# A two-layer encoder on one core: matmuls in runs by width, toeplitz biases in the grid biases' buffers, last halves by token half

## The chip, the core and the metric

The kernel runs on one core of a Trainium2 chip. The metric is the device time of one execution in microseconds (us), lower is better. Before the change it is 2096.45 us, the median of three runs (2096.22 to 2096.68).

## What is computed

The input is 256 tokens of 2048 float32 features. Each of two layers normalises, projects, attends, projects back with a residual, normalises again and applies a squared-ReLU MLP (2048 to 8192 to 2048) with a residual. A final normalisation ends it. Layer 0 has 16 heads of 128: eight with a neighbourhood on a 64-wide grid and a learned bias, eight with a mix of dilated bands. Layer 1 has 16 query heads on four key and value heads, a band of 128 tokens to each side and a sink in each head's softmax. Cut to what matters:

```python
for i in range(DEPTH):                      # 2
    h = rms_norm(x, attn_norm[i])
    if i % 2 == 0:
        x = x + even_mixer(h, even_w_in, even_rpb, even_w_out)   # grid heads | dilated heads
    else:
        x = x + odd_mixer(h, odd_w_qkv, odd_sink, odd_w_out)     # banded, with sink
    h = rms_norm(x, mlp_norm[i])
    a = relu(h @ w_mlp_in[i])
    x = x + (a * a) @ w_mlp_out[i]
return rms_norm(x, final_norm)
```

## The kernel before

**Two parts for each number.** Each float32 operand of a large product is split into a high part in a matmul format of TensorE (ScalarE, L90) and the rest, the low part (VectorE, L91). A product is high x high + high x low + low x high. The code calls the parts of a weight h and l; u holds both parts of the normalised input (feature-major: 16 k-tiles of 128 features, high then low, 256 tokens each), hid those of the MLP's hidden layer, o those of the attention's output.

**Units.** A unit makes 128 output features of a projection by features. For each of the 16 k-tiles there is a pair: h as the stationary operand against 512 columns, u high and low side by side (L143), and l against the 256 columns of u high (L141). Both accumulate in one PSUM tile, acc, of which there are three. `products` issues one pair and `k_range` loops over k; the order in the pair turns round on every odd k, so the widths go 512, 256, 256, 512, 512, 256, 256 and so on. A `tick` comes after every fourth pair. `two_units` holds back the last four k-tiles of two units until waiting work is done.

**Chunks.** A chunk makes 512 output columns of a product by tokens (the values, the output projections, the second MLP matrix). Here the weights are the moving operand, 512 wide, and the stationary operand is one of the two token halves of 128: for each k, and for each token half, three 512-wide matmuls (L185). Even chunks accumulate in acc, odd ones in s_ps. A chunk of the MLP has 32 k-tiles, two to a weight load.

**Weights.** `take_half` (L103 to L111) keeps loads of 512 KB ("halves") flowing: SP issues the load into raw (six buffers), ScalarE makes h and VectorE l (five buffers each).

**Order.** The program is written as one stream; small steps of the attention are put in by `later(steps, fn)`, due after so many ticks: scores (L296), then the softmax, transposes of the weights (L321), then the values (L340). LAGS_0, LAGS_1 and LAGS_END hold the steps between these. When the program is built, instructions are put on each engine's queue when their data and buffers are expected to be free; each engine then runs its queue strictly in order. So a step with few inputs can stand in a queue well ahead of its place in the code.

**Biases of layer 0.** The grid heads (0 to 7) get their bias from a table that GpSimd loads (rev, L533) and expands (rel, L538, four buffers). The other eight get a toeplitz bias, one VectorE operation on a constant table tabs (L374, tile toep, two buffers of 128x384). tabs is loaded by GpSimd behind the bias of head 4 (L543), and so are the rows of x for the residual (L547). Layer 1 uses the same function on another part of the table.

**Start.** TensorE is warmed by ten small products of ones (L467). Then gx (gains and x by features) and the first weights (`first`, four units' worth) come in alternating loads on SP, two k-tiles at a time (L482, L484), with k = 0 and k = 1 apart. Four units are computed side by side in four PSUM tiles, k outermost (L501 to L504). Each k-tile of u is made from gx by L200 (high) and L201 (low).

**End.** In the last chunk of layer 1's MLP all matmuls of both token halves finish together. Then `added` adds both halves (L397), squares follow on ScalarE (L206), `finish_norm` makes the scale of each token (L225 to L232), `scaled` applies it in eight pieces on ScalarE and VectorE (L426, L428, L430), and SP stores four column chunks of 512 KB, both token halves in each (L437).

Of the kernel before, what the change touches and what calls it, by code (L numbers as in the profile page):

```python
# [43 lines left out]
def encoder(ctx: ExitStack, tc: tile.TileContext, a: dict, out: bass.AP):  # L44
# [34 lines left out]

    nc.vector.memset(ones, 1.0)  # L80
# [56 lines left out]
    def products(ps, h, l, k, flip):  # L137

        for low in (flip, not flip):
            if low:  # L140
                nc.tensor.matmul(ps[:, :T], l, u[:, k, 0, :], start=False, stop=k == KT - 1 and not flip)  # L141
            else:
                nc.tensor.matmul(ps, h, u[:, k].rearrange("p a t -> p (a t)"), start=k == 0,  # L143
                                 stop=k == KT - 1 and flip)
# [25 lines left out]
    def chunk(act, nk, c, done, before=None):  # L170

        if c % 2 == 0:
            ps = [acc_ps.tile([P, NC], F32, name="acc") for _ in range(2)]
        else:
            ps = [aux_ps.tile([P, NC], F32, name="s_ps", bufs=2) for _ in range(2)]
        for k in range(nk):
            if k % 2 == 0:
                parts = [w.rearrange("p k c -> p (k c)") for w in take_half()]
            if before and k == nk - 2:
                before()  # L180
            h, l = (w[:, (k % 2) * NC:(k % 2 + 1) * NC] for w in parts)
            for j in range(2):
                js = slice(j * P, (j + 1) * P)
                for n, (x, y) in enumerate(((0, h), (0, l), (1, h))):
                    nc.tensor.matmul(ps[j], act[:, k, x, js], y, start=k == 0 and n == 0,  # L185
                                     stop=k == nk - 1 and n == 2)
            tick()
        done(c, ps)
# [35 lines left out]
    def finish_norm():  # L224
        nc.vector.tensor_reduce(ms, ssq, axis=AX.X, op=ALU.add)  # L225
        r0, v, e = (work.tile([P, 2], F32, name=n, bufs=1) for n in ("r0", "v", "e"))
        nc.scalar.activation(r0, ms, AF.Sqrt, bias=eps, scale=1.0 / D)
        nc.vector.tensor_scalar(v, ms, 1.0 / D, EPS, op0=ALU.mult, op1=ALU.add)
# [3 lines left out]
        nc.vector.scalar_tensor_tensor(rcol, e, 1.5, r0, op0=ALU.add, op1=ALU.mult)  # L232
# [40 lines left out]
    def value_quad(pool, keep):  # L273

        def done(_, ps):
            assert norm["ready"]
            w = pool.tile([P, 2, 2, NC], F32R, name="v", bufs=1)
            for j in range(2):
                nc.scalar.activation(w[:, 0, j, :], ps[j], AF.Copy, scale=rcol[:, j:j + 1])
                nc.vector.scalar_tensor_tensor(w[:, 1, j, :], ps[j], rcol[:, j:j + 1],  # L280
                                               w[:, 0, j, :].bitcast(F32), op0=ALU.mult, op1=ALU.subtract)
            keep.append(w)
        chunk(u, KT, 0, done)
# [67 lines left out]
    def project_out(o, which):  # L351
        def done(c, ps):
# [12 lines left out]
        for c in range(CHUNKS):  # L365
            chunk(o, KT, c, done, before if c == 0 else None)
            if c == 2:
                warm(AF.Sqrt, ssq[:, 0, 0:1])
        heads_done.clear()

    def toeplitz(pool, slope, which):
        def fn():
            t = pool.tile([P, TW], F32, name="toep", bufs=2)
            nc.vector.scalar_tensor_tensor(t, tabs[:, 0, :], -slope, tabs[:, which, :],  # L374
                                           op0=ALU.mult, op1=ALU.add)
            return [t[:, P - P * i:P - P * i + T] for i in range(2)]
        return fn

    def mlp(layer, which_next):
        with tc.tile_pool(name=f"mlp{layer}", bufs=1) as pool:  # L380
# [3 lines left out]
            for b in range(2):  # L384
# [9 lines left out]
                def added(c, ps):  # L394
                    cs = slice(c * NC, (c + 1) * NC)
                    for j in range(2):
                        nc.vector.scalar_tensor_tensor(xs[:, j, cs], ps[j], rsq[:, j:j + 1], xs[:, j, cs],  # L397
                                                       op0=ALU.mult, op1=ALU.add)
                    if b == 1 and which_next < 4:
                        to_features(c, which_next)  # L400
                    for j in range(2):
                        if b == 1:
                            squares(c, j)
                    if b == 1 and which_next == 4 and c < CHUNKS - 1:
                        nc.vector.tensor_mul(xs[:, :, cs], xs[:, :, cs],
                                             last_gain[:, None, cs].to_broadcast([P, 2, NC]))

# [12 lines left out]
    def last_norm(last_gain):  # L420
        finish_norm()

        def scaled(c, j, engine):
            y, r = xs[:, j, c * NC:(c + 1) * NC], rcol[:, j:j + 1]
            if c == CHUNKS - 1:
                nc.vector.scalar_tensor_tensor(y, y, r, last_gain[:, c * NC:], op0=ALU.mult, op1=ALU.mult)  # L426
            elif engine is nc.scalar:
                nc.scalar.activation(y, y, AF.Copy, scale=r)  # L428
            else:
                nc.vector.tensor_scalar(y, y, r, None, op0=ALU.mult)  # L430

        for c, engines in ((0, (nc.scalar, nc.scalar)), (3, (nc.vector, nc.vector)),
                           (1, (nc.vector, nc.scalar)), (2, (nc.vector, nc.vector))):
            cs = slice(c * NC, (c + 1) * NC)
            for j in range(2):
                scaled(c, j, engines[j])
            nc.sync.dma_start(out[:, :, cs], xs[:, :, cs])  # L437
# [28 lines left out]
    for _ in range(10):  # L466
# [5 lines left out]
    rs = []  # L472
# [4 lines left out]
    for k0 in range(0, KT, 2):  # L477
        r = raw.tile([P, 2, 4, P], F32, name="r")
        for k1 in ((k0 + 1, k0 + 2) if k0 == 0 else (k0 + 2,)):
# [4 lines left out]
            nc.sync.dma_start(r[:, ks.start - k0:ks.stop - k0], a["first"][:, ks])  # L484
# [3 lines left out]
        rs.append(r)  # L488
# [4 lines left out]
    nc.gpsimd.tensor_scalar(sink_neg, sink, -1.0, None, op0=ALU.mult)  # L493
    for k0 in range(0, KT, 2):
# [174 lines left out]
```

## Time and profile before

| | before |
|---|---|
| median of three runs | 2096.45 us |
| profiled execution, its own time | 2096.66 us |
| its span, first to last instruction | 2094.8 us |
| TensorE busy | 2066.0 us (99%) |
| VectorE, ScalarE, GpSimd busy | 1261.1, 1016.0, 23.4 us |
| TensorE's mean granted clock over the span | 0.995 |
| 512-wide matmuls of units, L143, outside the start | 2864 |
| their 256-wide partners, L141 | 2864 |
| 512-wide matmuls of the MLP's chunks, L185 on hid | 3072 |
| HBM read and written | 386.46 and 2.10 MB |

In the profile PE is TensorE's matmul and PEld its weight load, DVE is VectorE, ACT ScalarE, POOL GpSimd and SP the engine that issues most loads. Times are in us from the start of the span, unless marked ns. A timeline row has the start, the length, the engine, the line, the operation, the tile written and those read, the shape, and how many were merged (x2); in square brackets stands the engine's idle time just before and who ended it. A row of the waits has who waited, for whom, the total, the number of times and the longest. A row of the stretches has the stretch, its length, the busy time and count of engines, TensorE's granted clock (1.00 is full), the share of the DMA engines and the GB/s. The length of a matmul in the rows is from its start to the end of its results, longer than the distance to the next start; the spacing is read from the starts.

### The profile page before, as it was taken

The numbers are of one execution on the slowest core, as the hardware profiler recorded it, in microseconds if no ns is written. First come the engines' busy times: TensorE is split into PE (matmuls) and PEld (weight loads), VectorE is DVE, ScalarE is ACT, GpSimd is POOL, SyncE is SP. The second block draws the span as 40 slices with busy tenths as digits, with TensorE's granted clock in tenths as the row PEclk, the third lists the DMA queues.
The fourth block names the chain that finished last, engine by engine and source line by source line (L and its number), as shares of the span: only waits on it lengthen the run. The fifth ranks groups of instructions, "written<-read, shape, count | busy, mean of one in ns | idle before, by whom it ended". The sixth has DMA issues, their size and how long they took to land.

```text
span 2094.8 us, 27875 instructions
## 1 busy us (share of the span) xinstructions
PE 2066.0 (99%) x10712; PEld 1759.4 (84%) x10712; DVE 1261.1 (60%) x1777; ACT 1016.0 (48%) x1453; POOL 23.4 (1%) x42
## 2 busy tenths in 40 slices
PE   9799999999999999999999999999999999999997
PEld 7688888888888888888888888888888888888886
DVE  7567765566654456665545887566664446665453
ACT  7455555554543344554444655554543334544442
POOL 2200000000000000000000000000000000000000
PEclk9999999999999999999999999999999999999999
DMA  9655555555566655555555544565566665556662
GB/s 321 192 166 168 176 175 172 182 189 190 191 192 191 192 192 190 191 189 193 185 190 188 163 151 146 186 201 191 189 190 194 191 194 188 190 191 192 191 193 98
DMA packets 107812, 390.38 MB, mean 186 GB/s; under 512 B 12144, under 2 KB 12416, under 8 KB 107040
## 3 DMA queue, kind: packets, MB, share of 16 engines
q1 hardware_dynamic: 106496, 383.87, 57.4%
q0 software_dynamic: 1184, 4.74, 0.7%
q8 instruction: 84, 1.38, 0.3%
q14 instruction: 48, 0.39, 0.1%
HBM read 386.46 MB, written 2.10 MB: 185 GB/s over the span
## 4 chain that ended last, share of the span: by engine, by line
PE 97%; DMA 1%; POOL 0%; DVE 0%; ACT 0%; issue 0%; SPq 0%; DVEq 0%; POOLq 0%
PE acc L143 32%; PE acc L185 25%; PE s_ps L185 21%; PE acc L141 16%; PE m_ps L340 1%; PE s_ps L296 1%; DMA rev<-in_rpb 1%; PE p_ps L321 1%; PE m_ps L214 1%; POOL rel L538 0%; DMA r<-in_first 0%; DMA tabs<-in_tabs 0%; PE s_ps L143 0%; POOL rev L533 0%; DVE l L91 0%
## 5 line engine op out<-in xcount | busy, mean ns | idle before, releaser
L91 DVE TENSOR_TENSOR l<-r,h 128x1024 fp32r<-128x1024 f32 (+1 forms) x721 | 882.9, 1225 | 615.4 <-ACT h L90 602.9
L90 ACT ACTIVATE h<-r 128x1024 fp32r<-128x1024 f32 (+1 forms) x721 | 761.9, 1057 | 689.5 <-PE acc L185 274.5
L143 PE MATMUL acc<-u,h 128*128 128x512 f32 x2864 | 915.4, 396 | 1.3 <-ACT h L90 1.3
L141 PEld LDWEIGHTS acc<-u,l 128*128 128x128 f32 x2864 | 538.1, 188 | 125.0 <-DVE l L91 1.2
L141 PE MATMUL acc<-u,l 128*128 128x256 f32 x2864 | 566.4, 278 | 0.5 <-DVE l L91 0.5
L143 PEld LDWEIGHTS acc<-u,h 128*128 128x128 f32 x2864 | 442.8, 189 | 2.1 <-ACT h L90 1.6
L185 PE MATMUL s_ps<-h,hid 128*128 128x512 f32 x1024 | 318.3, 390 | 0.0
L185 PE MATMUL acc<-h,hid 128*128 128x512 f32 x1024 | 317.5, 389 | 0.0
L185 PEld LDWEIGHTS acc<-h,hid 128*128 128x128 f32 x1024 | 192.2, 188 | 39.9
L185 PEld LDWEIGHTS s_ps<-h,hid 128*128 128x128 f32 x1024 | 192.2, 188 | 39.8
L192 ACT ACTIVATE t<-acc 128x256 f32<-128x256 f32 x179 | 68.9, 385 | 292.6 <-PE acc L143 291.6
L185 PE MATMUL s_ps<-l,hid 128*128 128x512 f32 x512 | 199.2, 389 | 0.0
L185 PE MATMUL acc<-l,hid 128*128 128x512 f32 x512 | 199.2, 389 | 0.0
L194 DVE TENSOR_TENSOR z<-acc,t 128x256 f32<-128x256 f32 x179 | 75.9, 425 | 146.7 <-ACT t L192 146.3
L185 PEld LDWEIGHTS s_ps<-l,hid 128*128 128x128 f32 x512 | 96.1, 188 | 19.7
L185 PEld LDWEIGHTS acc<-l,hid 128*128 128x128 f32 x512 | 96.1, 188 | 19.7
L185 PE MATMUL acc<-h,u 128*128 128x512 f32 x320 | 102.9, 394 | 0.7 <-ACT h L90 0.7
L185 PE MATMUL acc<-h,o 128*128 128x512 f32 x256 | 82.9, 394 | 0.0
L185 PE MATMUL s_ps<-h,o 128*128 128x512 f32 x256 | 82.7, 395 | 0.0
L185 PEld LDWEIGHTS acc<-h,u 128*128 128x128 f32 x320 | 59.8, 188 | 13.0 <-ACT h L90 1.0
L185 PE MATMUL acc<-l,u 128*128 128x512 f32 x160 | 62.6, 391 | 0.5 <-DVE l L91 0.5
L390 DVE SCALAR_TENSOR_TENSOR z<-z 128x256 f32<-128x256 f32 x128 | 54.4, 425 | 4.3
(100 smaller groups left out, 1027.6 us busy)
## 6 DMA issues: line engine op xcount, KB each, us to landing
r<-in_w_mlp_in SPq DMA_DIRECT2D x256, 512.0 KB, 4.1
r<-in_w_mlp_out SPq DMA_DIRECT2D x256, 512.0 KB, 3.7
r<-in_even_w_in SPq DMA_DIRECT2D x56, 512.0 KB, 3.8
r<-in_odd_w_qkv SPq DMA_DIRECT2D x40, 512.0 KB, 3.8
r<-in_even_w_v SPq DMA_DIRECT2D x32, 512.0 KB, 3.7
r<-in_even_w_out SPq DMA_DIRECT2D x32, 512.0 KB, 3.6
r<-in_odd_w_out SPq DMA_DIRECT2D x32, 512.0 KB, 3.6
r<-in_odd_w_v SPq DMA_DIRECT2D x8, 512.0 KB, 3.6
```

What stands on the lines that cost most here:

```text
L90: nc.scalar.activation(hi, src, AF.Copy)
L91: nc.vector.tensor_sub(lo, src, hi.bitcast(F32))
L141: nc.tensor.matmul(ps[:, :T], l, u[:, k, 0, :], start=False, stop=k == KT - 1 and not flip)
L143: nc.tensor.matmul(ps, h, u[:, k].rearrange("p a t -> p (a t)"), start=k == 0, stop=k == KT - 1 and flip)
L185: nc.tensor.matmul(ps[j], act[:, k, x, js], y, start=k == 0 and n == 0, stop=k == nk - 1 and n == 2)
L192: nc.scalar.activation(t, ps[:, T:], AF.Copy)
L194: nc.vector.tensor_add(z, ps[:, :T], t)
L214: nc.tensor.transpose(ps[:, k, j * P:(j + 1) * P], xs[:, j, (k0 + k) * P:(k0 + k + 1) * P], ident)
L296: nc.tensor.matmul(s_ps[:, i, :], qh[:, x, qs], kh[:, y, :], start=n == 0, stop=n == 2)
L321: nc.tensor.transpose(p_ps[:, j, i * P:(i + 1) * P], s[:, i, j * P:(j + 1) * P], ident)
L340: nc.tensor.matmul(o_ps[:, :T], vv[:, x, j, side * P:(side + 1) * P], pt[:, y, j, :], start=n == 0, stop=n == 5)
L390: nc.vector.scalar_tensor_tensor(z, z, 0.0, z, op0=ALU.max, op1=ALU.mult)
```

## The change

Four things are done.

1. `products` takes a list of pairs and issues all matmuls of one width, then all of the other, with a tick behind each. `k_range` gives it eight k-tiles at a time: the first eight high (512 wide) first, the second eight low (256 wide) first. So a unit is 8 high, 16 low, 8 high. At the start one call covers two k-tiles of the four units, high first for k = 0 and 1, low first for k = 2 and 3, and so on in turn.
2. Toeplitz biases of layer 0 take a buffer of the name rel, with four buffers, in the place of toep. Layer 1 keeps toep.
3. In the last chunk of the program, the last four halves (eight k-tiles) are taken all four, and their products made for the first token half, which is then finished (added, squared, normalised, stored), and then for the second. `finish_norm` works on one token half's column. The output of each token half leaves in two stores: the upper 1024 columns by SP, the lower ones by ScalarE's queue. The columns 0 to 1023 are scaled by ScalarE, the others by VectorE.
4. The very first weight load is issued by ScalarE's queue, as its first instruction. Eight products of ones are made in the place of ten.

```diff
+    r = raw.tile([P, 2, 4, P], F32, name="r")
+    nc.scalar.dma_start(r[:, 0:1], a["first"][:, 0:1])
+    rs = [r]
     nc.vector.memset(ones, 1.0)
...
-    def products(ps, h, l, k, flip):
-
-        for low in (flip, not flip):
-            if low:
-                nc.tensor.matmul(ps[:, :T], l, u[:, k, 0, :], start=False, stop=k == KT - 1 and not flip)
-            else:
-                nc.tensor.matmul(ps, h, u[:, k].rearrange("p a t -> p (a t)"), start=k == 0,
-                                 stop=k == KT - 1 and flip)
+    def products(banks, tiles, k, low_first, last):
+
+        for low in (low_first, not low_first):
+            for n, (ps, (h, l)) in enumerate(zip(banks, tiles)):
+                stop = last and low != low_first and (k[n] == KT - 1)
+                if low:
+                    nc.tensor.matmul(ps[:, :T], l, u[:, k[n], 0, :], start=False, stop=stop)
+                else:
+                    nc.tensor.matmul(ps, h, u[:, k[n]].rearrange("p a t -> p (a t)"), start=k[n] == 0, stop=stop)
+            tick()
 
     def k_range(ps, parts, ks):
-        for k in ks:
-            h, l = parts[k]
-            products(ps, h, l, k, k % 2 == 1)
-            if k % 4 == 3:
-                tick()
+        for k0 in range(ks.start, ks.stop, HALF):
+            k = range(k0, min(k0 + HALF, ks.stop))
+            products([ps] * len(k), [parts[i] for i in k], k, k0 >= HALF, True)
...
-    def chunk(act, nk, c, done, before=None):
+    def chunk(act, nk, c, done, before=None, apart=0):
...
-        for k in range(nk):
+        for k in range(nk - 2 * apart):
...
+        if apart:
+            kept = [take_half() for _ in range(apart)]
             for j in range(2):
-                js = slice(j * P, (j + 1) * P)
-                for n, (x, y) in enumerate(((0, h), (0, l), (1, h))):
-                    nc.tensor.matmul(ps[j], act[:, k, x, js], y, start=k == 0 and n == 0,
-                                     stop=k == nk - 1 and n == 2)
-            tick()
-        done(c, ps)
+                for k in range(nk - 2 * apart, nk):
+                    some(kept[(k - nk) // 2], k, (j,))
+                done(c, ps, (j,))
+        else:
+            done(c, ps, range(2))
...
     def toeplitz(pool, slope, which):
         def fn():
-            t = pool.tile([P, TW], F32, name="toep", bufs=2)
+
+            if which == 1:
+                t = pool.tile([P, 6, GRID], F32, name="rel", bufs=4).rearrange("p j c -> p (j c)")
+            else:
+                t = pool.tile([P, TW], F32, name="toep", bufs=2)
...
-                    chunk(hid, 2 * KT, c, added)
-            if which_next == 4:
-                last_norm(last_gain)
+                    chunk(hid, 2 * KT, c, added, apart=4 if which_next == 4 and b == 1 and c == CHUNKS - 1 else 0)
+
+    def last_norm(j, last_gain):
+
+        finish_norm(slice(j, j + 1))
+        r = rcol[:, j:j + 1]
+        for c in range(CHUNKS):
+            y = xs[:, j, c * NC:(c + 1) * NC]
             if c == CHUNKS - 1:
                 nc.vector.scalar_tensor_tensor(y, y, r, last_gain[:, c * NC:], op0=ALU.mult, op1=ALU.mult)
+            elif c == CHUNKS - 2:
+                nc.vector.tensor_scalar(y, y, r, None, op0=ALU.mult)
+            else:
                 nc.scalar.activation(y, y, AF.Copy, scale=r)
+        nc.sync.dma_start(out[:, j, D // 2:], xs[:, j, D // 2:])
+        nc.scalar.dma_start(out[:, j, :D // 2], xs[:, j, :D // 2])
...
-    for _ in range(10):
+    for _ in range(8):
         nc.tensor.matmul(wps[:, :P], ones, ones, start=True, stop=True)
...
+            if k1 > 1:
+                nc.sync.dma_start(r[:, ks.start - k0:ks.stop - k0], a["first"][:, ks])
...
-        for k in range(k0, k0 + 2):
-            for i in range(4):
-                products(sps[i], h[:, k - k0, i, :], l[:, k - k0, i, :], k, k > 0 and i % 2 == 1)
+        which = [(k, i) for k in range(2) for i in range(4)]
+        products([sps[i] for _, i in which], [(h[:, k, i, :], l[:, k, i, :]) for k, i in which],
+                 [k0 + k for k, _ in which], k0 % 4 == 2, True)
```

More of the change, by code (lines that the diff above doesn't have):

```diff
@@ L222, in encoder, with finish_norm @@
     norm = {"ready": False, "waiting": []}
[L224 to L228, printed above, removed]
+    def finish_norm(js=slice(0, 2)):
+        r0, v, e = (work.tile([P, 2], F32, name=n, bufs=1)[:, js] for n in ("r0", "v", "e"))
+        m, r = ms[:, js], rcol[:, js]
+        nc.vector.tensor_reduce(m, ssq[:, js], axis=AX.X, op=ALU.add)
+        nc.scalar.activation(r0, m, AF.Sqrt, bias=eps, scale=1.0 / D)
+        nc.vector.tensor_scalar(v, m, 1.0 / D, EPS, op0=ALU.mult, op1=ALU.add)
         nc.vector.reciprocal(r0, r0)
@@ L273, in value_quad, with done @@
     def value_quad(pool, keep):
-        def done(_, ps):
+        def done(_, ps, js):
             assert norm["ready"]
@@ L351, in project_out, with done @@
     def project_out(o, which):
-        def done(c, ps):
+        def done(c, ps, js):
             cs = slice(c * NC, (c + 1) * NC)
@@ L392, in hidden, with added @@
                     return fn
-                def added(c, ps):
+                def added(c, ps, js):
                     cs = slice(c * NC, (c + 1) * NC)
-                    for j in range(2):
+                    for j in js:
                         nc.vector.scalar_tensor_tensor(xs[:, j, cs], ps[j], rsq[:, j:j + 1], xs[:, j, cs],
                                                        op0=ALU.mult, op1=ALU.add)
-                    if b == 1 and which_next < 4:
+                    if b == 0:
+                        return
+                    if which_next < 4:
                         to_features(c, which_next)
[L401 to L404, printed above, removed]
+                    for j in js:
+                        squares(c, j)
+                    if which_next == 4 and c < CHUNKS - 1:
                         nc.vector.tensor_mul(xs[:, :, cs], xs[:, :, cs],
                                              last_gain[:, None, cs].to_broadcast([P, 2, NC]))
+                    elif which_next == 4:
+                        last_norm(js[0], last_gain)
                 for j in range(0, 2 * KT, 2):
@@ L493, in encoder @@
     nc.gpsimd.tensor_scalar(sink_neg, sink, -1.0, None, op0=ALU.mult)
+    assert not tasks
     for k0 in range(0, KT, 2):
```

34 lines of the change are left out of this document (14 added, 20 removed).

## The prediction

> **What bounds the kernel now.** I read the page first. Its first lines and the chain by engine:
>
> ```profile
> span 2094.8 us, 27875 instructions
> PE 2066.0 (99%) x10712; PEld 1759.4 (84%) x10712; DVE 1261.1 (60%) x1777; ACT 1016.0 (48%) x1453; POOL 23.4 (1%) x42
> PE 97%; DMA 1%; POOL 0%; DVE 0%; ACT 0%; issue 0%; SPq 0%; DVEq 0%; POOLq 0%
> ```
>
> TensorE carries 97% of the chain, so only three things can move the time: the spacing of its matmuls, the places where it stands still, and what is left when it has ended. For the spacing I read the chain in order of time (start, length, what) and one group of the page:
>
> ```profile
> 146.73 1.43 PE m_ps L340 x12
> 721.24 43.52 PE s_ps L185 x192
> 943.10 43.52 PE acc L185 x192
> ```
>
> ```profile
> L141 PEld LDWEIGHTS acc<-u,l 128*128 128x128 f32 x2864 | 538.1, 188 | 125.0 <-DVE l L91 1.2
> ```
>
> In a chunk all matmuls are 512 wide: 43.52/192 = 0.2267 us each. Twelve 256-wide ones in a row take 1.43/12 = 0.119. Between the chunks (721.24 + 43.52 = 764.76, and 943.10) lie the 32 units of the second half of layer 0's MLP: 178.34/32 = 5.573 us for one unit's 16 pairs of 512 (h) and 256 (l). At the uniform prices it would be 16 x 0.2267 + 16 x 0.119 = 5.531. So the present order, with eight changes to 256 and back per unit, costs 0.042 us a unit. The group, the weight loads of the 256-wide matmuls, gives the number of pairs outside the start: 2864, or 179 units.
>
> For the stillstands I read the waits, which hold one large one for TensorE, and around it the timelines of the engines concerned:
>
> ```profile
> PE m_ps L340 <- DVE v L280: 11.0, 1, 11.0
> DVE toep L374 <- DMA tabs<-in_tabs: 12.0, 1, 12.0
> ```
>
> ```profile
> 59.72 0.40 PE L340 MATMUL m_ps<-pt,v 128*128 128x256 f32 x2
> 71.16 2.52 PE L340 MATMUL m_ps<-pt,v 128*128 128x256 f32 x10 [11.04 <-DVE v L280]
> ```
>
> ```profile
> 55.07 0.61 DVE L314 TENSOR_SCALAR s<-s,rd 128x256 f32<-128x256 f32 x2
> 67.68 0.56 DVE L374 SCALAR_TENSOR_TENSOR toep<-tabs 128x384 f32<-128x384 f32 x1 [12.01 <-DMA tabs<-in_tabs]
> 68.15 1.22 DVE L91 TENSOR_TENSOR l<-r,h 128x1024 fp32r<-128x1024 f32 x1
> 69.29 0.69 DVE L91 TENSOR_TENSOR pt<-p_ps,pt 128x512 fp32r<-128x512 f32 x1
> ...
> 70.35 1.41 DVE L280 SCALAR_TENSOR_TENSOR v<-acc,rcol,v 128x512 fp32r<-128x512 f32 x2
> ```
>
> VectorE's queue is in order, and a toeplitz bias of head 8, used much later, stands in it at 55.7 us, waiting for the table, whose load was issued only then:
>
> ```profile
> 63.15 0.57 POOL L543 DMA_DIRECT2D tabs<-in_tabs  x1
> ```
>
> Behind it stand an l split, a pt and the value split v, for which TensorE waits. The stretches of TensorE (busy, count, granted clock) show a second price:
>
> ```profile
> 59.90:64.30 4.40, 0.22 (x2) 1.00 0.06 11
> 64.30:71.10 6.80, 0.00 (x0) 0.50 0.99 368
> 71.10:74.60 3.50, 3.44 (x14) 0.50 0.76 261
> ```
>
> After 4.4 idle us the clock was at half, and stayed so through 3.44 us of matmuls.
>
> **The change part by part.** *Toeplitz in the grid buffers.* What put L374 so early? A free buffer: the trace shows a later one directly behind the last read that frees its buffer.
>
> ```profile
> 118.78 0.09 DVE L301 DVE_READ_ACCUMULATOR2_ANT st<- 128x1 f32 x1
> ...
> 192.80 0.08 DVE L301 DVE_READ_ACCUMULATOR2_ANT st<- 128x1 f32 x1
> 192.92 0.56 DVE L374 SCALAR_TENSOR_TENSOR toep<-tabs 128x384 f32<-128x384 f32 x1
> ```
>
> Now it has to have one of the four grid buffers, and heads 4 to 7, ahead of it in the code, claim them first; head 8 gets the buffer of head 4, which is read to 118.8 (the first row), 50 us behind the landing of the table. The 59.96 to 71.16 hole, 11.2 us, goes, and half of 3.44 us at half clock, less what the partial start hid: 1.6. What is late next? ScalarE's half of v:
>
> ```profile
> 57.84 1.38 ACT L279 ACTIVATE v<-acc,rcol 128x512 fp32r<-128x512 f32 x2 [0.56 <-PE acc L185]
> ```
>
> The first v tile is there at about 58.55; VectorE, free from 55.7, has had 2.9 us by then for the l split and the pt (1.22 + 0.69), and has the low half of the first v at 59.3 and of the second at 60.0 (1.41 for both). TensorE wants the first at 59.96 and the second at 60.3. I take the whole 12.8; between the ends 11.2 (clock price not returned) and 12.8.
>
> *Runs by width.* A unit becomes 8 h, 16 l, 8 h, so 16 of each width in a row across units, with one change and back instead of eight. What does one cost when the runs are long? The nearest place is a block of six 256s between 512s:
>
> ```profile
> 128.99 0.88 PE L296 MATMUL s_ps<-k,q 128*128 128x256 f32 x6
> 129.70 0.39 PE L185 MATMUL acc<-h,u 128*128 128x512 f32 x1
> ...
> 130.86 0.62 PE L185 MATMUL acc<-h,u 128*128 128x512 f32 x2
> ```
>
> Five 512s start from 129.70 to before 130.86: 1.16 us, against 5 x 0.2267 = 1.133: the first ones behind a narrow run are slower by 0.027 together. So one change and back costs 0.03 here and 0.042/8 = 0.005 in the present mixture. A unit becomes 5.531 + 0.005 to 0.03 = 5.536 to 5.561, and 179 units save 6.6 to 2.1 us. The inserted block is nearer to a long run than the mixture: 2.5 us. Were 256s a little dearer in long runs (0.120), it would be none.
>
> The Trainium skill (TensorE: Matmul & The Clock Gate, Back-to-back issue gap) gives an isolated gap of N/2.4 + 2.5 ns whatever stands beside the matmul. By it the order is worth nothing, and the sum below is 2.5 us smaller; this trace has 227 ns where it gives 216.
>
> Ticks stay four to a unit but fall behind 8 h (1.81 us) or 8 l (0.95), not every 1.39; each lag of the attention shifts by at most 0.45 us. I put no cost, 0 to 2 us for the range. The insertions of six now fall between runs of the two widths.
>
> *Start.* TensorE waits here for the second weights (rows in time; the first is the load that changes queue):
>
> ```profile
> 1.18 0.42 SPq L484 DMA_DIRECT2D r<-in_first  x1
> 9.25 1.06 ACT L90 ACTIVATE h<-r 128x1024 fp32r<-128x1024 f32 x1 [0.33 <-DMA r<-in_first]
> 10.34 1.23 DVE L91 TENSOR_TENSOR l<-r,h 128x1024 fp32r<-128x1024 f32 x1 [0.90 <-ACT h L90]
> 10.36 0.73 PE L143 MATMUL acc<-u,h 128*128 128x512 f32 x2 [1.30 <-ACT h L90]
> 11.62 0.50 PE L141 MATMUL acc<-u,l 128*128 128x256 f32 x2 [0.53 <-DVE l L91]
> ```
>
> With k = 2, 3 low first, TensorE starts at the end of L91 (11.6), not of L90: one idle stretch of 2.5 us instead of 1.30 + 0.53. Against that SP issues one load less, so this chain moves up by about 0.4; ScalarE, which now issues that load ahead of its table load, has nothing to do before 3 us. The eight warm-ups instead of ten end earlier, and the wait covers it. Net zero, from -0.8 to +1.
>
> *End.* Rows of the last chain:
>
> ```profile
> 2081.26 1.43 DVE L397 SCALAR_TENSOR_TENSOR gx<-s_ps,rsq,gx 128x512 f32<-128x512 f32 x2 [10.60 <-PE s_ps L185]
> 2082.80 0.63 ACT L206 ACTIVATE sq<-gx 128x512 f32<-128x512 f32 x1
> 2084.67 0.16 DVE L232 SCALAR_TENSOR_TENSOR rcol<-e,r 128x2 f32<-128x2 f32 x1
> 2084.87 1.95 ACT L428 ACTIVATE gx<-gx,rcol 128x512 f32<-128x512 f32 x3 [0.82 <-DVE rcol L232]
> 2084.87 1.42 DVE L426 SCALAR_TENSOR_TENSOR gx<-gx,rcol,last_gain 128x512 f32<-128x512 f32 x2
> 2086.28 3.53 SPq L437 DMA_DIRECT2D out<-gx  x4
> ```
>
> and stretches of the stores (length, clock, DMA share, GB/s):
>
> ```profile
> 2088.30:2089.40 1.10, 0.50 1.02 382
> 2093.50:2094.80 1.30, 0.50 0.00 0
> ```
>
> The second L397 starts with the end of the matmuls (2081.9), and the steps to rcol stay as long for one column. Then 2 MB leave at 382 GB/s, 1.38 us per 512 KB. The first half's chain takes the same 4.4 us (2081.9 to 2086.28), but starts 24 x 0.2267 = 5.4 us before the end of the matmuls; its two stores, issued 1 us before that end, are gone before the second half's are issued 4.4 us behind it. So two stores remain of four: 2 x 1.38 = 2.8 us less, and VectorE's two scalings, one of them the shorter kind without the gain, release the first issue up to 0.2 earlier. Two queues share the one path: no more. 3.0, from 2.6 to 3.3. ScalarE issues its first store between its scalings and the second squares, 1 us before they are due; nobody waits. The four kept halves fit the five buffers; their splits are long done (VectorE idle 10.60 above).
>
> Sum: 12.8 + 2.5 + 0 + 3.0 = 18.3. The profiled execution took 2096.66 us (span 2094.8 and 1.9 around it), the median 2096.45: 2078.4 and 2078.2.
>
> **The rivals.** (1) *Order is free*, as by the rule above: 2078.2 + 2.5 = 2080.7. For it: 256s that grow to 0.120. (2) *The toeplitz still gets in early*, into a free grid buffer ahead of head 5's bias: two of four are free at 55 us, since only heads 0 and 1 have been read. Against: the code claims head 5's first. The 12.8 stay: 2091.0. (3) *The 512s do not settle*: the five above average 0.232; if all do, a unit is 5.531 + 16 x 0.0053 = 5.616, 0.043 over now, 7.7 us: 2078.2 + 2.5 + 7.7 = 2088.4. Against: the chunk rows settle. (4) *The start's idle stretch halves the clock*. 4.4 us did, 1.3 did not; 2.1 to 2.5 lies between. The low clock lasted 10.3 us (64.3 to 74.6); half of that is 5.1: 2083.3. The Trainium skill (same page, The HAM clock gate) asks for a whole idle window of 3.4 us; the trace agrees so far. (5) *Slower: weight loads bound the runs of l*. A load is recorded at 0.188 us (the group above), longer than the 0.119 of the matmul that must cover it. Twelve in a row ran well; if from the thirteenth on each takes 0.188, a unit pays 4 x 0.069 = 0.276, 49 us in all: 2080.7 + 49 = 2130. It decides from 15.8/179 = 0.088 us a unit, two such matmuls.
>
> **How the numbers follow.** Forecast 65%, (1) 14%, (2) 9%, (3) 5%, (4) 5%, (5) 2%. The forecast's own ends are 2078.2 - 4.1 (runs at 6.6) - 0.8 - 0.3 = 2073, and 2078.2 + 2.5 + 1 + 2 + 0.4 = 2084. Range 2072 to 2086: it takes in (1) and (4), and leaves out (2), (3), (5), 16%, and some tail. 0.2% is 4.2 us, about what a measurement of this kernel can tell from no change. Faster by that: all but (5) and the poor ends of (2) and (3): 0.93; within it 0.05; slower 0.02.
>
> **What would show it.** No wait of VectorE on the table, L374 first behind 100 us, TensorE without a hole at 60 to 71 us and the clock at full from 7 us to the end; a second-half MLP of 177.2 to 178.0 us between the chunks instead of 178.34; one hole near 9 to 11.6 us, no longer than 2.6; from the last matmul to the end of the span 10 us instead of 12.9. The prediction is wrong if a hole above 1 us stands at the first values, if the stretch of units is longer than now, or if the stores still queue behind one another for more than two transfers.

## The result, and the profile after

Four runs of the changed kernel took 2079.56 us in the median (2079.34 to 2082.51), beside 2096.56 (2096.22 to 2099.78) for the kernel before. The ratio is 0.9919, with a 95% interval of 0.9902 to 0.9936: 17.0 us less, where the forecast was 18.3. The profiled execution took 2079.34 us with a span of 2077.2, that is 2.1 us around the span where the kernel before had 1.9.

The first lines of the page of after and its chain by engine:

```profile
span 2077.2 us, 27861 instructions
PE 2063.3 (99%) x10708; PEld 1767.9 (85%) x10708; DVE 1257.6 (61%) x1782; ACT 1014.3 (49%) x1455; POOL 27.8 (1%) x42
PE 99%; DMA 0%; ACT 0%; DVE 0%; SPq 0%; issue 0%
```

TensorE now carries 99% of the chain instead of 97%. Its busy time fell by only 2.7 us: most of the gain is time in which it stood still.

Where the time went can be read by following one and the same matmul through both traces, since the products outside the start and the last halves stand in nearly the same order. The table gives the starts, in us:

| matmul | before | after | gained so far |
|---|---|---|---|
| first product of the start | 5.33 | 5.17 | 0.16 |
| first matmul of the first value chunk | 31.68 | 30.88 | 0.80 |
| first unit behind that chunk | 58.33 | 58.36 | -0.03 |
| first matmul of the next value chunk | 121.68 | 108.89 | 12.79 |
| last matmul of all | 2081.52 | 2067.58 | 13.94 |
| end of the span | 2094.84 | 2077.19 | 17.65 |

**The hole.** The timelines of VectorE and of TensorE in after, around the first values, and one row of the stretches (length, busy time and count of TensorE, clock, DMA share, GB/s):

```profile
57.64 0.68 DVE L94 TENSOR_TENSOR pt<-p_ps,pt 128x512 fp32r<-128x512 f32 x1
58.59 1.44 DVE L296 SCALAR_TENSOR_TENSOR v<-acc,rcol,v 128x512 fp32r<-128x512 f32 x2 [0.28 <-ACT v L295]
```

```profile
58.36 1.99 PE L148 MATMUL acc<-u,h 128*128 128x512 f32 x8
60.19 1.60 PE L356 MATMUL m_ps<-pt,v 128*128 128x256 f32 x12
61.63 2.08 PE L146 MATMUL acc<-u,l 128*128 128x256 f32 x16
```

```profile
59.70:71.20 11.50, 11.50 (x73) 1.00 0.69 213
```

VectorE reaches the value split at 58.59, with 0.28 us of waiting for ScalarE, where it did so at 70.35 before. The products of the weights with the values, now L356, run from 60.19 without a gap. The toeplitz biases, now L394, come much later. The row has the shortest, median and longest duration in ns and the first and last start in us:

```profile
L394 DVE SCALAR_TENSOR_TENSOR rel<-tabs x8: 535/558/560, 106.3 to 241.1; 128x384 f32<-128x384 f32 x8
```

**Runs by width.** The chain of after, in order of time, around the second half of layer 0's MLP:

```profile
708.13 43.52 PE s_ps L186 x192
755.38 3.65 PE acc L148 x16
760.94 3.65 PE acc L148 x16
766.51 3.65 PE acc L148 x16
...
929.78 43.52 PE acc L186 x192
```

Sixteen 512s in a row take 3.65 us, and a unit 760.94 - 755.38 = 5.56. By the starts of the matmuls the 32 units take 178.13 us, where they took 178.34.

**The clock at the start.** Stretches of after, cut where its granted clock can change:

```profile
8.85:12.26 3.41, 2.16 (x13) 1.00 1.04 407
29.33:32.74 3.41, 1.87 (x8) 1.00 0.74 289
32.74:36.15 3.41, 3.41 (x10) 0.50 0.79 250
36.15:39.57 3.42, 3.42 (x16) 1.00 0.73 215
```

The clock was at half from 32.74 to 36.15 us, which is new in this place. What leads to it are two waits at the beginning of the first value chunk:

```profile
30.88 0.73 PE L186 MATMUL acc<-h,u 128*128 128x512 f32 x2 [1.01 <-ACT h L93]
32.13 0.50 PE L186 MATMUL acc<-l,u 128*128 128x512 f32 x1 [0.53 <-DVE l L94]
```

**The end.** Rows of the timeline of after:

```profile
2068.00 0.75 DVE L417 SCALAR_TENSOR_TENSOR gx<-s_ps,rsq,gx 128x512 f32<-128x512 f32 x1 [1.45 <-PE s_ps L186]
2070.64 0.16 DVE L248 SCALAR_TENSOR_TENSOR rcol<-e,r 128x1 f32<-128x1 f32 x1
2070.84 1.33 ACT L452 ACTIVATE gx<-gx,rcol 128x512 f32<-128x512 f32 x2 [0.81 <-DVE rcol L248]
2071.24 0.74 DVE L448 SCALAR_TENSOR_TENSOR gx<-gx,rcol,last_gain 128x512 f32<-128x512 f32 x1
2072.21 0.34 ACTq L454 DMA_DIRECT2D out<-gx  x1
```

and the groups of the stores, first of before (duration of the issue in ns, first and last start), then of after:

```profile
L437 SPq DMA_DIRECT2D out<-gx x4: 602/724/1218, 2086.3 to 2088.6; - x4
DMA to landing us min/median/max: 3.2/4.2/5.0
```

```profile
L453 SPq DMA_DIRECT2D out<-gx x2: 343/344/344, 2066.6 to 2072.0; - x2
L454 ACTq DMA_DIRECT2D out<-gx x2: 338/342/347, 2066.8 to 2072.2; - x2
DMA to landing us min/median/max: 2.6/3.2/3.7
```

The last matmul ends at 2067.97, and the span 9.23 us later, where it was 12.93.

### The profile page after: what moved, and what is told of

The parts are those of the page before. It is cut to its first block, busy times and chain, and to the rows that moved or that the text cites. A ratio compares the mean times of both kernels' runs of the same rounds, so it can differ in the third digit from the quotient of the medians.

```text
span 2077.2 us, 27861 instructions
## 1 busy us (share of the span) xinstructions
PE 2063.3 (99%) x10708; PEld 1767.9 (85%) x10708; DVE 1257.6 (61%) x1782; ACT 1014.3 (49%) x1455; POOL 27.8 (1%) x42
## 3 DMA queue, kind: packets, MB, share of 16 engines
q8 instruction: 84, 1.38, 0.3%
## 4 chain that ended last, share of the span: by engine, by line
PE 99%; DMA 0%; ACT 0%; DVE 0%; SPq 0%; issue 0%
PE acc L148 31%; PE acc L186 26%; PE s_ps L186 21%; PE acc L146 16%; PE s_ps L312 1%; PE m_ps L356 1%; PE p_ps L337 1%; PE m_ps L229 1%; DMA r<-in_first 0%; PE s_ps L148 0%; DVE l L94 0%; ACT h L93 0%; PE s_ps L146 0%; ACT gx L452 0%; SPq L500 0%; PE m_ps L259 0%
## 5 line engine op out<-in xcount | busy, mean ns | idle before, releaser
L148 PE MATMUL acc<-u,h 128*128 128x512 f32 x2864 | 694.2, 391 | 0.3 <-DVE u L216 0.3
L148 PEld LDWEIGHTS acc<-u,h 128*128 128x128 f32 x2864 | 524.1, 188 | 100.4 <-ACT h L93 0.6
L146 PEld LDWEIGHTS acc<-u,l 128*128 128x128 f32 x2864 | 366.9, 191 | 14.0 <-DVE l L94 1.9
L146 PE MATMUL acc<-u,l 128*128 128x256 f32 x2864 | 377.0, 283 | 1.7 <-DVE l L94 1.7
```

Of the source, the lines that this page charges most:

```text
L146: nc.tensor.matmul(ps[:, :T], l, u[:, k[n], 0, :], start=False, stop=stop)
L148: nc.tensor.matmul(ps, h, u[:, k[n]].rearrange("p a t -> p (a t)"), start=k[n] == 0, stop=stop)
```

## The experiments

The theory: the hole was one blocked queue and goes whole; the order of the widths is worth what each change from one width to the other costs, which the runs can measure; the end is one path of bytes; and the start moves by a clock that falls after a thin stretch. The rivals: the hole's gain is partly due to something else; the order is free; the end is set by a price per store; the start's loss comes from the new order of products in it. Beside the times, each kernel's trace is compared matmul by matmul with that of before, since one execution's start differs from the next by more than a microsecond.

**The toeplitz buffers alone**, in the kernel before:

```diff
-            t = pool.tile([P, TW], F32, name="toep", bufs=2)
+            if which == 1:
+                t = pool.tile([P, 6, GRID], F32, name="rel", bufs=4).rearrange("p j c -> p (j c)")
+            else:
+                t = pool.tile([P, TW], F32, name="toep", bufs=2)
```

> The kernel before with one edit alone: layer 0's toeplitz biases take a buffer of the name rel. My theory: the whole hole of TensorE at 60 to 71 us came from the bias standing early in VectorE's queue, so it goes with this edit alone, and the half-clock stretch behind it: 2096.6 - 12.8 = 2083.8 us, no wait of VectorE on the table, and the next stages unmoved. Rival: a part of the 12.8 us in the changed kernel came from the new tick places or from the start (other edits); then a hole or a wait above 0.5 us stays near 60 us here, and the time is above 2084.5.

Measured: 2084.30 us (2083.18 to 2085.35), beside 2097.80 for the kernel before; ratio 0.9936 (0.9920 to 0.9953), 13.5 us. In the trace the step across the hole is 12.84 us; from there on no stage differs by more than 0.03. So edit 2 alone gives the 12.8, and the hole's price is independent of the other edits. One thing was not foreseen: the first value chunk began 1.60 us later than before, although the start of this kernel is the old one. Its stretches:

```profile
8.16:11.57 3.41, 1.70 (x8) 1.00 1.01 378
11.57:14.99 3.42, 3.21 (x11) 0.50 1.04 414
32.05:35.47 3.42, 2.17 (x10) 1.00 0.34 123
```

Here the clock fell at the first wait of the start, with code that kept it at full in the trace of before, and stayed at full behind the second (the third row). The fall is thus no property of the new order.

**The change with the old order of the widths**, in the units and at the start:

```diff
...
     def k_range(ps, parts, ks):
...
+        for k in ks:
+            h, l = parts[k]
+            products(ps, h, l, k, k % 2 == 1)
+            if k % 4 == 3:
+                tick()
...
```

> The changed kernel with the old order of pairs in units and at the start (512, 256, 256, 512), and the old places of the ticks. My theory, from the step table of the two traces: the second-half MLP stretch between the chunks goes back from 178.13 to 178.34 us, 1.2 us over all units, and the start is equal to within 0.3 us: 2079.6 + 1.2 = 2080.8. Rival: the runs gave nothing (a second cause, such as moved attention steps, gave the 0.21 us); then the stretch stays at 178.13 and the time at 2079.6.

Measured: 2079.38 us (2079.10 to 2081.36), ratio 0.9916 (0.9901 to 0.9931). By the total, the order is worth nothing; by the trace it is worth something. The units of the second half of the MLP are back at 178.3 us, the hole's step is 12.83 and the end's 3.70, but the clock never fell in this execution, and the first unit behind the first value chunk came 0.84 us earlier than before, against 0.03 later in after. So the start gave 0.87 of the 1.15 us back that the old order takes, and hid the widths. A total of one kernel with 1 to 2 us of chance in its start can't tell an edit of 1 us; the stage can.

**Changing the width at every matmul**, 512, 256, 512, 256, in the units and at the start:

```diff
-            products([ps] * len(k), [parts[i] for i in k], k, k0 >= HALF, True)
...
+            products(ps, h, l, k, False)
...
```

> The changed kernel with units in strict alternation: 512, 256, 512, 256 and so on. Theory of the transient: the first 256 behind a 512 is short (113 ns where 120 is settled) and the first 512 behind a 256 long (233 where 227 is), and the dear ones are the second to fifth 512 behind a change (236, 228, 233, 231), which this order never reaches: 346 ns a pair, a unit of 5.54 us instead of 5.567, 179 units 5 us less: 2074.5. Rival, a fixed price of some 20 ns for each change to 256 and back, as one long run of the changed kernel pays: 16 of them a unit, 5.87 us a unit, +54 us: 2133. Between them, the price in the old mixture (3.3 ns for each change and back over the settled spacings): 5.60 a unit, +6 us: 2085.5.

Measured: 2091.64 us (2088.95 to 2092.12), ratio 0.9970 (0.9959 to 0.9982). The timeline of TensorE in the units shows every matmul by itself:

```profile
799.83 0.40 PE L146 MATMUL acc<-u,h 128*128 128x512 f32 x1
800.06 0.28 PE L144 MATMUL acc<-u,l 128*128 128x256 f32 x1
800.18 0.40 PE L146 MATMUL acc<-u,h 128*128 128x512 f32 x1
800.41 0.28 PE L144 MATMUL acc<-u,l 128*128 128x256 f32 x1
```

By the starts in the trace, a pair takes 0.3533 us, 0.0066 more than one 512 and one 256 in long runs; a unit takes 5.653. So a change and back costs 6.6 ns in this pattern. None of the three expected times came: not 2074.5 (the dear places never reached), not 2133 (20 ns for every change), and 6 us more than the 2085.5 between them. The price of a change depends on how long the runs are.

**Runs of 32**: the MLP's units are taken two at a time, all 512s of both, then all 256s:

```diff
+        for low in (False, True):
+            for i in range(2):
+                for k in range(KT):
+                    ...
-                        unit(hidden(j))
-                        unit(hidden(j + 1))
+                        pair([hidden(j), hidden(j + 1)])
```

> The changed kernel with the MLP's units taken two at a time: 16 wide matmuls of the one, 16 of the other, then 16 and 16 narrow ones, so that runs are 32 long. Theory: a long run pays 20 ns for its change to 256 and back whatever its length (the first narrow one is 7 ns short, five wide ones are 28 long), so a unit pays half: 5.567 - 0.010 = 5.557 us, 178.13 - 0.32 = 177.8 us in the second-half MLP stretch, 1.3 us over the 128 MLP units. Rival: holding four halves at a time starves the splits (five buffers each), and TensorE waits at the changes of width; then the stretch is longer than 178.13.

Measured: 2078.23 us (2076.52 to 2078.69), beside 2096.45; ratio 0.9911 (0.9894 to 0.9927). Rows of its chain, one line for the 512s and one for the 256s:

```profile
752.18 7.25 PE acc L171 x32
759.44 3.83 PE acc L169 x32
763.27 7.28 PE acc L171 x32
770.55 3.83 PE acc L169 x32
774.38 7.28 PE acc L171 x32
```

Two units take 774.38 - 763.27 = 11.11 us, and the 32 units of the stretch 177.79, by the starts, against 178.13 in runs of 16. The starts of single matmuls in these runs, in ns from one to the next and averaged over 14 runs, settle this point. A run of 512s goes 233, 236, 228, 233, 231 and then 226.7 to its end; a run of 256s goes 113, 119 and then 120.0 to its end. The five first 512s cost 28 ns more than settled ones, the two first 256s 8 ns less: a change and back costs 20 ns, and a unit in long runs 16 x 0.2267 + 16 x 0.1200 = 5.547 us without changes. Runs of 16 have one change a unit: 5.567, as measured (178.13/32). Runs of 32 have half of one: 5.557, or 177.8 for 32 units, as measured. The old order, in runs of two, has eight at (5.573 - 5.547)/8 = 3.3 ns.

**Filling the second gap of the start**: eight products whose result nobody reads, behind the last two k-tiles of the start:

```diff
+    for i in range(8):
+        nc.tensor.matmul(wps[:, :T], l[:, 1, i % 4, :], u[:, KT - 1, 0, :], start=True, stop=True)
```

> The changed kernel with eight 256-wide matmuls behind the first four units, whose result nobody reads, to keep TensorE busy in the gap ahead of the first value chunk (29.9 to 30.9 us). In the changed kernel the granted clock fell to half from 32.7 to 36.2 us behind this gap, which it did not before. Theory: the gap and the next one left TensorE less than half busy in one window, and the half clock ate what the start had gained (0.8 us): without it the value chunk ends 0.8 us earlier and the time is 2078.8. Rival: the first attention scores wait for another chain anyway (TensorE stood 0.86 us there before, 0.1 after): the clock stays full but the time stays at 2079.6.

Measured: 2078.85 us (2077.77 to 2080.85), ratio 0.9913 (0.9898 to 0.9927). In the profiled execution the filled gap kept the clock, and the other gap lost it:

```profile
8.69:12.10 3.41, 1.60 (x12) 1.00 1.03 404
12.10:15.52 3.42, 3.42 (x10) 0.50 1.05 425
32.58:36.00 3.42, 2.83 (x13) 1.00 0.21 68
```

The median is the 2078.8 that was expected, but this execution doesn't show the expected way to it: the stretch behind the filled gap took 1.63 us less than in after, and the first value chunk began 2.16 us later. Two of the four executions took 2077.8 us, the other two 2079.9 (this one) and 2080.9.

**Filling both gaps**: the same eight products also behind the first two k-tiles.

```diff
+        if k0 in (0, KT - 2):
+            for i in range(8):
+                nc.tensor.matmul(wps[:, :T], l[:, 1, i % 4, :], u[:, k0 + 1, 0, :], start=True, stop=True)
```

> The changed kernel with eight unread narrow matmuls in each of the two gaps of the start, behind k = 1 and behind k = 15. In the profiles so far the clock fell to half for 3.41 us behind windows of that length in which TensorE streamed 0.34 and 0.36 of the time (near 10 or near 31 us), and stayed full behind windows with 0.44 and more; where the windows begin differs from run to run. Theory: with both gaps filled no window is below 0.44, the clock is full in every run, and the executions lie near 2078.0 us, closer together than those of the changed kernel (2079.3 to 2082.5). Rival: the executions scatter by another cause; then the spread stays, and the median stays above 2079.

Measured: 2079.08 us (2078.39 to 2080.64), ratio 0.9919 (0.9904 to 0.9933). The clock stayed at full throughout, yet the first unit behind the first value chunk gained only 0.22 us on before. So the clock isn't the whole of the start's chance: its loads and the products put in take part too, and what each takes is open. The median stayed above 2079, as the rival had it, and is not told apart from that of the change.

**Both gaps filled and runs of 32** together:

> Both gaps of the start filled and the MLP's runs 32 long, the two expected gains together: 2079.6 - 1.3 - 1.5 = 2076.8 us, the fastest version so far. Rival: as for the two alone; with the splits starved it is slower than the kernel with the filled gaps only.

Measured: 2077.05 us (2076.56 to 2077.76), ratio 0.9908 (0.9893 to 0.9923), span 2074.7. No clock fell here either, and that unit came 1.21 us earlier than before, with the same start as in the last kernel, where it was 0.22.

**One queue for the stores**, in the changed kernel:

```diff
-        nc.scalar.dma_start(out[:, j, :D // 2], xs[:, j, :D // 2])
+        nc.sync.dma_start(out[:, j, :D // 2], xs[:, j, :D // 2])
```

> The changed kernel with both stores of a token half issued by SP. In the changed kernel the last 512 KB land 7.98 us behind the last matmul, 3.69 earlier than before: 0.32 by an earlier first issue, 0.54 because the first store takes 2.62 us from issue to landing instead of 3.16, 2.83 because one more store follows it instead of three. Theory: the queue is not what shortens it, the two stores share the same DMA engines: 2.6 and 1.3 us again, the end of the span 9.2 us behind the last matmul, within 0.3. Rival: the second queue gave the 0.54 or more: the end comes 0.5 to 1 us later here.

Measured in a single execution: 2081.45 us, span 2079.6. The time is that of a bad start: the clock fell at 13.71 us behind a thin stretch, and the first unit behind the first value chunk came 2.33 us later than before. The end is what the kernel was made for, and it took 9.30 us from the end of the matmuls against 9.23: the last store was issued 0.31 us later than from ScalarE's queue and landed 0.06 later. The second queue buys next to nothing.

**Four stores for each token half**, in the fastest kernel, and **one store for each**, in the changed kernel:

```diff
-        nc.sync.dma_start(out[:, j, D // 2:], xs[:, j, D // 2:])
-        nc.scalar.dma_start(out[:, j, :D // 2], xs[:, j, :D // 2])
+        for c in (2, 0, 3):
+            nc.sync.dma_start(out[:, j, c * NC:(c + 1) * NC], xs[:, j, c * NC:(c + 1) * NC])
+        nc.scalar.dma_start(out[:, j, NC:2 * NC], xs[:, j, NC:2 * NC])
```

> The fastest kernel so far (both start gaps filled, runs of 32), with each token half's output in four stores of 256 KB instead of two of 512 KB: SP issues three, each as soon as its column chunk is scaled, ScalarE's queue the last. Two theories of the end, where the second of two stores lands 1.31 us behind the first. Bytes: all stores share one path of 512 KB in 1.31 us, behind a delay of 2.62 - 1.31 = 1.3 us from issue to first byte. The first chunk of the second token half is scaled 3.4 us behind the end of the matmuls, so the first of four lands at 3.4 + 1.3 + 0.66 = 5.4, the last at 5.4 + 3 x 0.66 = 7.3 instead of 8.0, and the end comes 8.6 us behind the last matmul's end instead of 9.25: time 2077.05 - 0.65 = 2076.4 us. Per store: the 1.31 us are a price of each store, whatever its size: the last of four lands at 5.4 + 3 x 1.31 = 9.3, the end at 10.6: 2078.4 us. The start varies by 1 us between executions, so the end is read from the trace.

```diff
-        nc.sync.dma_start(out[:, j, D // 2:], xs[:, j, D // 2:])
-        nc.scalar.dma_start(out[:, j, :D // 2], xs[:, j, :D // 2])
+        nc.sync.dma_start(out[:, j], xs[:, j])
```

> The changed kernel with each token half's output in one store of 1 MB, issued by SP behind all four scalings. Bytes: issued 4.24 us behind the end of the matmuls, landed 1.3 + 2 x 1.31 = 3.9 later, at 8.2, and the end at 9.4 instead of 9.23. Per store: landed 2.62 behind its issue, at 6.9, and the end at 8.1. What the start does between executions does not touch this; it is read from the trace.

The groups of the stores, in quarters and then whole:

```profile
L469 SPq DMA_DIRECT2D out<-gx x6: 332/377/404, 2063.6 to 2069.9; - x6
L470 ACTq DMA_DIRECT2D out<-gx x2: 356/360/364, 2064.4 to 2069.9; - x2
DMA to landing us min/median/max: 2.0/2.7/3.2
```

```profile
L453 SPq DMA_DIRECT2D out<-gx x2: 343/346/348, 2065.8 to 2071.3; - x2
DMA to landing us min/median/max: 3.9/3.9/3.9
```

A store that finds the path free lands 2.0 us behind its issue with 256 KB, 2.6 with 512 KB and 3.9 with 1 MB: 1.4 us and about 1.25 for every 512 KB. So bytes set the end, and a price per store is out. The whole store landed 8.21 us behind the end of the matmuls, as reckoned by bytes; the quarters' last landed at 7.49 instead of 7.3. From the last landing to the end of the span it was 1.24 us in after, 1.38 with whole stores and 1.50 with quarters, so that of the 0.65 us expected of the quarters 0.27 were left (8.98 behind the end of the matmuls, from 9.25). What that last stretch consists of wasn't taken apart. In quarters the kernel took 2076.67 us (2076.22 to 2077.68), beside 2096.35; ratio 0.9903 (0.9885 to 0.9921), the fastest median of all, 2.9 us under that of the change. Against the same kernel with two stores it isn't told apart by the totals.

## Why the prediction was right, and where it was off

The time lay 1.4 us above the forecast, inside its range. Step by step:

**The hole** was forecast at 12.8 and gave 12.82 in the change and 12.84 by itself. Reading the price of a stall with the half clock that follows it, 11.2 + 1.6, was right. So was the argument on who is late next: ScalarE's half of v, by 0.28 us. Rival 2, a toeplitz bias that still gets in early, fell with the first one at 106.3 us, behind 100 as forecast.

**Runs by width** were forecast at 2.5, with a second-half MLP of 177.2 to 178.0 us; it took 178.13, and the steps of the units sum to 1.15. The step that failed is the uniform price of a 256, "Twelve 256-wide ones in a row take 1.43/12 = 0.119". That mean holds the two quick ones at the head of a run, 113 and 119 ns; the settled price is 0.120. Sixteen cost 1.912, not 1.904. The other half of the step was right: five 512s that are 27 ns slower together, read from an inserted block, are the 28 of the runs. The prediction named its weak point, 256s at 0.120, and concluded "it would be none". That was too much, as the two quick ones come back in every run. Rival 1, a free order, is refuted. Between runs of 16 and pairs the totals can't tell; by turns they can, with 2091.64 us against 2079.38 for pairs, and the traces show where it lies: a unit goes from 5.567 to 5.653, which would be 15.4 us over 179 units, and from the first unit behind the first value chunk to the last matmul it is 14.1 us more than in after. The Trainium skill (TensorE: Matmul & The Clock Gate, Back-to-back issue gap) gives an isolated gap of N/2.4 + 2.5 ns, in which only the width N stands. By that formula the order would be free; the traces don't agree, in the order or in the gap, which settles at 226.7 ns here against 215.8.

Rival 3 and rival 5 fell too: the 512s settle from the sixth on, and the 256s stay at 120 ns through 32 in a row, although a weight load is recorded at 191 ns.

```profile
L146 PEld LDWEIGHTS acc<-u,l 128*128 128x128 f32 x2864 | 366.9, 191 | 14.0 <-DVE l L94 1.9
```

The recorded length of a load is longer than the distance between two of them, so it is no bound.

**The start** was forecast at net zero, from -0.8 to +1, and the first unit behind the first value chunk came 0.03 later than before. That is the right number for the wrong reason: 0.80 was gained up to 30.88 us and lost again in the stretch of the half clock. Rival 4 had the mechanism, but in another place and at another price. The single wait, 1.69 us to 10.10, did not halve the clock in this execution; the two waits at 30.88 and 32.13 did. And the price was not 5.1 us. From the first value chunk to the next unit after took 27.49 us, 0.83 more than before. Three other traces have the same code there and the same two waits, but no fall behind them (whole stores, one queue, runs of 32), and took 25.84 to 25.86. So the fall cost 1.6 us, and without it the start would have gained 1.6. The low clock lasted one stretch of 3.41 us, not three, since TensorE was busy in it, and half of 3.41 is the most that it can take.

```profile
10.10 0.63 PE L146 MATMUL acc<-u,l 128*128 128x256 f32 x3 [1.69 <-DVE l L94]
```

The two waits in the kernel with whole stores, where the clock stayed at full behind them:

```profile
31.57 0.73 PE L186 MATMUL acc<-h,u 128*128 128x512 f32 x2 [1.01 <-ACT h L93]
32.82 0.50 PE L186 MATMUL acc<-l,u 128*128 128x512 f32 x1 [0.53 <-DVE l L94]
```

**The end** was forecast at 3.0, from 2.6 to 3.3, and gave 3.71. The two stores fewer were right: 2.83 us by the landings, against 2.8. Two small terms were missed. The first store of the second half was issued 4.05 us behind the end of the matmuls, not 4.37, so 0.32 earlier instead of "up to 0.2". And the prediction took it that a store lands as long behind its issue as before; the group of the stores has 3.2 us as the least before and 2.6 after. The issue itself takes 0.34 us instead of 0.60 at the least, which is about half of that. The queue isn't the reason, as one queue gave 2.6 as well, and the length of a row isn't either, as the issue takes 0.33 to 0.40 us with rows of 2, 4 and 8 KB. What is left is the number of rows, 256 in a store before and 128 after; that is argued, not tried.

The sum: 12.82 + 1.15 - 0.03 + 3.71 = 17.65 us of span. In the time it is 2096.66 - 2079.34 = 17.32, since what lies around the span grew from 1.9 to 2.1 us. Among the experiments it was either 1.8 to 1.95 or 2.1 to 2.2, without a pattern that follows the edits; that stays open.

## What to carry to other kernels

Look for an operation that stands early in an in-order queue because its buffer happens to be free: its wait is paid by everything behind it, and a buffer that comes free later delays it; here that took 12.8 us off and cost nothing that a trace shows. Price a pattern of instructions from single spacings in the trace, head and tail of a run apart, and not from the mean of a short run. Where the start of a kernel differs by 1 to 2 us from one execution to the next, judge an edit of 1 us by its own stage in the trace and not by the total.

## What the runs showed of the hardware

**The clock falls behind a stretch that is only thin.** The granted clock changes at points 3.41 us apart, which lie differently in each execution. For each such window of the start, in the twelve traces of this case, the share in which TensorE was fed can be worked out: each matmul counts from its start for its settled spacing, 0.2267 us for a 512 and 0.120 for a 256 at full clock, cut at the window's edges, and the sum is taken over 3.41. Behind shares of 0, 0.33, 0.37, 0.38, 0.39 and 0.39 the clock was at half in the next window; behind 0.42, 0.45, 0.46, 0.46, 0.47, 0.47, 0.47 and all higher ones it stayed. After is the 0.387 of these. The nearest of these that stayed, 0.419, is the kernel with whole stores at the end, in the same place of the same start:

```profile
29.52:32.93 3.41, 1.87 (x8) 1.00 0.89 338
32.93:36.30 3.37, 3.37 (x15) 1.00 0.59 184
```

Its busy time, 1.87 us, is just that of after (29.33 to 32.74), so the busy time of the rows, which has the ends of matmuls in it, doesn't tell the two apart; the fed share puts them on both sides of a line near 0.4. The windows at the end of the kernel, where the matmuls run out, come nearer still. Behind 0.33 there (both gaps filled) the clock was at half, behind 0.46 (one queue) it stayed, and behind 0.401 (second gap filled) it stayed too, against the 0.394 behind which it fell at the start of that same kernel. The row of the 0.401 and the one after it:

```profile
2066.93:2070.34 3.41, 1.53 (x7) 1.00 0.72 287
2070.34:2073.75 3.41, 0.00 (x0) 1.00 0.18 71
```

Windows so close don't prove the line, and the share depends on how a matmul across an edge is counted: by the matmuls that start in the window, after and the kernel with whole stores both have 0.398. But counted as above, all windows lie on the right side of it. The length of a wait doesn't decide: a single one of 2.25 us (whole stores, to 10.79 us) kept the clock, and 1.39 and 0.53 us (toeplitz buffers alone) lost it. What a wait does depends on where the window's edge falls in it, and that differs with each execution. The Trainium skill (TensorE: Matmul & The Clock Gate, The HAM clock gate) has the clock fall after at least one idle window of about 3.4 us and calls the window free-running. The traces agree with the length and the free running, and not with the idle: windows fed to 0.33 to 0.39 were enough. Its one busy window back to full agrees (32.74 to 36.15 in after).

**A change of width has a transient of five matmuls**, of 233, 236, 228, 233 and 231 ns for 512s, and of two, of 113 and 119, for 256s. In runs of one, two and 16 or 32 a change and back costs 6.6, 3.3 and 20 ns. Runs of two are the cheapest for each change, long ones the cheapest in sum: 106, 26, 20 and 10 ns a unit for runs of 1, 2, 16 and 32.
